# A gated recurrence in eight levels: its decay factors multiplied up beforehand, and GpSimd's product ordered behind VectorE's

## The chip, the cores and the metric

One NeuronCore of a Trainium2 chip runs the whole program. [...] The metric is the device time of one execution in microseconds (us); each kernel is timed several times and the median is taken.

## The reference, cut to what matters

One layer of a hybrid encoder block on 512 tokens of width 2048, in float32: an input norm, one wide projection, two token mixers, sigmoid gates, two projections merged, an output projection into the residual and a final norm. Mixer A, which the change touches, is a gated linear recurrence over 8 heads of 128:

```python
def step(state, inp):                       # one chunk of CHUNK tokens, g_c = log f
    q_c, k_c, g_c, v_c = inp
    cum = jnp.cumsum(g_c, axis=1)
    inter = jnp.einsum('bthk,bhkv->bthv', q_c * jnp.exp(cum), state)
    diff = cum[:, :, None] - cum[:, None, :]
    decay = jnp.exp(jnp.where(causal[None, :, :, None, None], diff, -jnp.inf))
    scores = jnp.einsum('bthk,bshk,btshk->bhts', q_c, k_c, decay)
    intra = jnp.einsum('bhts,bshv->bthv', scores, v_c)
    last = cum[:, -1]
    new_state = (jnp.exp(last)[..., None] * state
                 + jnp.einsum('bshk,bshv->bhkv', k_c * jnp.exp(last[:, None] - cum), v_c))
    return new_state, inter + intra
```

So a query at t meets a key at s with the product of the forget factors f between them. Mixer B is a sparse attention: an indexer scores all keys, the best 128 of them are kept for each query (top-k), and attention over those carries a position bias.

## The kernel before, in words

Nearly all the time goes into the projections. Their weights come from HBM in blocks (`wr`); ScalarE rounds a block to its high half (`wh`) and VectorE subtracts that for the low half (`wl`), and TensorE makes three matmuls of each product of halves. All other work is written as Python generators in "lanes" (`hgrn` for mixer A's recurrences, `top` for the top-k, `att` for the attention, `norm` and so on). The projection loops call `pump()` after some of their matmuls, and each `pump()` lets every lane emit its next piece. Nothing is reordered afterwards: the order in which pieces are emitted is the order of the instructions on each engine.

`hgrn_gen(p)` is one recurrence; it handles two heads (p = 3, 2, 0, 1 in the order of time). It holds q, k and f of two heads as tiles of 128 x 1024 (channels x 2 heads x 512 tokens: `hq`, `hk`, `hf`). The decay between a query and a key is not computed pair by pair but in levels 0 to 7. At level l, m = 2^(l-1) tokens make a half block. `scores(l, ps)` multiplies keys and queries as they stand into PSUM (`hl`, 16 to 64 small matmuls). Then `decay(l)` multiplies the later half of each block of q by the factor of the earlier half, on VectorE, and the earlier half of each block of k by the factor of the later half, on GpSimd, so that the next level's scores carry the right decay. The factors are in `tot`: one for each half block; neighbours multiplied together give the `tot` of the next level, half as long (512, 256, ... 8 columns). Level 0 has only the product of q with f, on VectorE. For levels below 6 VectorE then copies by a mask from PSUM into `hnear`; later levels are copied into `hS` by ScalarE. After level 7 the keys are transposed (`hkt`), chunk states are built (`hp`, `hst`; these use the last `tot`), outputs are made (`ho`) and normed (`hz`).

Between two levels stands one `yield`, so one pump: about 24 projection matmuls on TensorE.

The lane `top` is for VectorE alone: rounds of MAX and MATCH_REPLACE over 256, 384 or 512 columns of `M`. It is paced by `R.load`, the number of microseconds that the piece of the recurrence just emitted is reckoned to take on VectorE:

```python
while credit <= 0:
    yield
    credit += 2.7 - R.load
credit -= 0.4 + 0.27 * (b + 1)
```

Other names of the steps: `nt`, `ckh`, `ckl` (norm lane, during the first recurrence: a product on VectorE, its rounding on ScalarE, the difference on VectorE), `ak`, `av`, `aq` and `MB` (attention, during the last recurrence: `MB` is a sum of the bias on GpSimd).

Of the kernel before, what the change touches and what calls it, by code (L numbers as in the profile page):

```python
# [26 lines left out]
F32 = mybir.dt.float32  # L27
FR = mybir.dt.float32r
AF = mybir.ActivationFunctionType
OP = mybir.AluOpType  # L30
# [20 lines left out]
def hybrid_block(ctx, tc, x, norm_w, w_in, lb_table, gnorm_a, q_norm_w, kv_norm_w, w_uq,  # L51
# [3 lines left out]
    V, A, G, PE, SP = nc.vector, nc.scalar, nc.gpsimd, nc.tensor, nc.sync  # L55
# [12 lines left out]
    def bank(name):  # L68
        return sdp.tile([128, 512], F32, name=name, tag="sd")

    def split(hi, lo, src):
        A.activation(hi, src, AF.Copy)  # L72
        V.tensor_tensor(lo, src, hi.bitcast(F32), op=OP.subtract)  # L73
# [6 lines left out]
    def mm(ps, l, r, first, last):  # L80
        PE.matmul(ps, l, r, start=first, stop=last, skip_group_check=True)  # L81
# [34 lines left out]
    R = SimpleNamespace(load=0.0)  # L116
# [564 lines left out]
    def place(p, shape, dtype, name, tag):  # L681
        if p == 1 or tag not in ("hf", "hk", "hq"):
            return R.h.tile(shape, dtype, name=name, tag=tag)
        return R.i.tile(shape, dtype, name=name, tag=f"{tag}{p or 3}")
# [58 lines left out]
    def aq_evac(p):  # L743
        def evac(c, ps):
            if c == 0:
                hg[p, "q"] = place(p, [128, 2, T], F32, "hq", "hq")
            q = hg[p, "q"][:, c, :]
            A.activation(q, ps, AF.Sigmoid)
            V.scalar_tensor_tensor(q, ps, 128 ** -0.5, q, op0=OP.mult, op1=OP.mult)
            if c == 1:  # L750
                lanes["hgrn"].append(hgrn_gen(p))
        return evac

    def hgrn_gen(p):
        f, k, q = (hg[p, n] for n in "fkq")
        gate = R.h.tile([128, 2, T], F32, name="hg")
        SP.dma_start(gate, gate_d[2 * p:2 * p + 2].rearrange("f p t -> p f t"))
        S = R.h.tile([128, 8, 128], F32, name="hS")
        near = R.h.tile([128, 8, 32], F32, name="hnear")
        G.memset(near, 0.0)  # L760
        qf, kf, tot = (a.rearrange("p c t -> p (c t)") for a in (q, k, f))
        yield

        def scores(l, ps):

            m = max(32, 1 << l >> 1)
            for n in range(8):
                for h in range(0, 128, m if l < 6 else 2 * m):
                    s = n * 128 + h
                    t = s if l < 6 else s + m  # L770
                    mm(ps[h:h + m, n * m:n * m + m], kf[:, s:s + m], qf[:, t:t + m], True, True)

        def decay(l):
            if l == 0:
                V.tensor_tensor(qf, qf, tot, op=OP.mult)
                return tot
            m = 1 << (l - 1)
            nb = 1024 // (2 * m)
            qv = qf.rearrange("p (n a m) -> p n a m", a=2, m=m)
            kv = kf.rearrange("p (n a m) -> p n a m", a=2, m=m)  # L780
            tv = tot.rearrange("p (n a) -> p n a", a=2)
            V.tensor_tensor(qv[:, :, 1, :], qv[:, :, 1, :],
                            tv[:, :, 0:1].to_broadcast([128, nb, m]), op=OP.mult)
            G.tensor_tensor(kv[:, :, 0, :], kv[:, :, 0, :],
                            tv[:, :, 1:2].to_broadcast([128, nb, m]), op=OP.mult)
            nt = R.h.tile([128, nb], F32, name=f"tot{l}", tag=f"tot{l % 2}")
            V.tensor_tensor(nt, tv[:, :, 0], tv[:, :, 1], op=OP.mult)
            return nt

        for l in range(8):  # L790
            R.load = (1.7, 2.5, 2.1, 1.8, 1.8, 1.7, 1.3, 1.3)[l]
            if l == 4:
                G.memset(S, 0.0)
            ps = bank("hl")
            scores(l, ps)
            tot = decay(l)
            if l < 6:
                V.copy_predicated(near, R.levels[:, l:l + 1, :].to_broadcast([128, 8, 32]),
                                  ps[:, 0:256].rearrange("p (n t) -> p n t", n=8))
            else:  # L800
                m = 1 << (l - 1)
                for h in range(0, 128, 2 * m):
                    A.activation(S[h:h + m, :, h + m:h + 2 * m],
                                 ps[h:h + m, 0:8 * m].rearrange("p (n t) -> p n t", n=8), AF.Copy)
            if l == 6:
                for h in range(0, 128, 32):
                    A.activation(S[h:h + 32, :, h:h + 32], near[h:h + 32], AF.Copy)
            yield

        R.load = 0.0  # L810
        kd = R.h.tile([128, 2, 3, 128], F32, name="hkd")
        for c in range(2):
            pt = bank("hkt")
            for j in range(3):
                PE.transpose(pt[:, j * 128:(j + 1) * 128], k[:, c, j * 128:(j + 1) * 128], R.ident)
            A.activation(kd[:, c], pt[:, :384].rearrange("p (j t) -> p j t", j=3), AF.Copy)
        yield
        while (p, "v") not in hg:
            yield
        R.load = 1.4  # L820
        v = hg[p, "v"]
        st = R.h.tile([128, 2, 3, 128], F32, name="hst")
        for c in range(2):
            pp = bank("hp")
            for j in range(3):
                mm(pp[:, j * 128:(j + 1) * 128], kd[:, c, j, :], v[:, j, c * 128:(c + 1) * 128],
                   j == 0, True)
            A.activation(st[:, c, 0, :], pp[:, 0:128], AF.Copy)
            for j in (1, 2):
                V.scalar_tensor_tensor(st[:, c, j, :], st[:, c, j - 1, :],  # L830
                                       tot[:, c * 4 + j:c * 4 + j + 1],
                                       pp[:, j * 128:(j + 1) * 128], op0=OP.mult, op1=OP.add)
        yield
        sq = place(p, [128, 2, T], F32, "hk", "hk")
        zs = []
        o = place(p, [128, 2, T], F32, "ho", "hf")
        for c in range(2):
            po = bank("ho")
            for j in range(4):
                sl = slice(j * 128, (j + 1) * 128)  # L840
                mm(po[:, sl], v[:, j, c * 128:(c + 1) * 128], S[:, 4 * c + j, :], j == 0, j == 0)
                if j:
                    mm(po[:, sl], st[:, c, j - 1, :], q[:, c, sl], False, True)
            A.activation(o[:, c], po, AF.Copy)
            A.activation(sq[:, c], po, AF.Square)
            R.load = 0.7 * c
            yield
            zs.append((place(p, [128, T], FR, "hzh", ("hkd", "hst")[c]),
                       place(p, [128, T], FR, "hzl", ("hq", "hS")[c])))
            split(*zs[c], sq[:, c])  # L850
        R.load = 0.7
        yield
        R.load = 0.0
        for c in range(2):
            ps = bank("hz")
            mm(ps, ones_r, zs[c][0], True, False)
            mm(ps, ones_r, zs[c][1], False, True)
            A.activation(sq[:, c], ps, AF.Ln, bias=eps, scale=1.0 / 128)
        A.activation(sq, sq, AF.Exp, scale=-0.5)
        yield  # L860
        R.load = 2.9
        for c in range(2):
            r = sq[:, c]
            V.scalar_tensor_tensor(r, o[:, c], c_gw, r, op0=OP.mult, op1=OP.mult)
            V.tensor_tensor(r, r, gate[:, c], op=OP.mult)
        yield
        R.load = 1.3
        for c in range(2):
            y = [place(p, [128, T], FR, f"hy{i}", (("hkd", "hst"), ("hq", "hS"))[i][c]) for i in range(2)]
            split(*y, sq[:, c])  # L870
            for i in range(2):
                late[1].append(lambda y=y[i], i=i, h=2 * p + c: SP.dma_start(ya_d[i, h], y.bitcast(F32)))
        yield


    at_ = {}

    def uq_evac(p):
# [323 lines left out]
    def end_index():  # L1202
        lanes["misc"].extend(waiting)
        drain("misc")
        leave("idx")
        leave("raws")
        R.h = enter("hgrn", side="right")
        lanes["hgrn"].extend((hgrn_gen(3), hgrn_gen(2)))
        lanes["norm"].append(norm_gen(R.ckv, 2, c_kvw, R.ckh, R.ckl))
        lanes["t5"].append(t5_gen())  # L1210
# [355 lines left out]
```

## Time and profile before

| | |
|---|---|
| median of 3 runs | 1365.66 us (1365.21 to 1366.12) |
| the profiled execution | 1364.76 us, of which the span from the first to the last instruction 1362.9 us |
| granted TensorE clock | 0.999 |
| TensorE, weight loads, VectorE, ScalarE, GpSimd busy in the span | 1347.1, 1250.5, 1075.5, 656.9, 81.5 us |

The four recurrences run beside projections. The first scores of each start at 685.5, 749.6, 810.0 and 883.1 us, and the last scores of the last one start at 910.6 us. The rows of a timeline below give start, length, engine, line, operation, tiles and shapes of an instruction, and in brackets how long its engine was idle before it and which instruction ended that. On VectorE the next instruction often starts some 0.07 us before the one ahead of it ends. Matmul rows of one kind are merged.

### The profile page before, as it was taken

Reading aid. Unit: us, or ns where it says so; the run is one execution under the profiler, and the core shown is the slowest. Engines: PE = TensorE matmul, PEld = TensorE weight load, DVE = VectorE, ACT = ScalarE, POOL = GpSimd, SP = SyncE. Lnnn points to the kernel's source line nnn. Section 1 sums busy time; section 2 is a strip of 40 time slices with the busy share of each in tenths; the row PEclk is TensorE's granted clock in tenths of the full one; section 3 lists DMA queues with packets and bytes.
Section 4 is the critical chain, followed back from the end, with each engine's and each line's share of the span. In section 5 each row is a group of like instructions: output and inputs, shape, how many; then the busy total and the mean of one; then the engine's idle time right before and its main releaser. Section 6 shows DMA issues by size and latency. Waiting matters only on the chain.

```text
span 1362.9 us, 26828 instructions
## 1 busy us (share of the span) xinstructions
PE 1347.1 (99%) x10940; PEld 1250.5 (92%) x10940; DVE 1075.5 (79%) x1741; ACT 656.9 (48%) x1054; POOL 81.5 (6%) x85
## 2 busy tenths in 40 slices
PE   8999999999999999999999999999999999999997
PEld 7888999999999999999999888888888888899996
DVE  7896889988898888886779989575556658899856
ACT  6555445445554444445744443645434334354444
POOL 2100000000000000000030303040101100000000
PEclk9999999999999999999999999999999999999999
DMA  6334345544444445446235423434856556643463
GB/s 207 94 109 139 98 151 160 164 142 140 131 148 117 133 139 155 140 140 206 63 103 153 127 80 109 134 108 149 299 163 204 197 174 219 209 145 119 164 239 139
DMA packets 145165, 204.79 MB, mean 150 GB/s; under 512 B 10585, under 2 KB 87058, under 8 KB 144914
## 3 DMA queue, kind: packets, MB, share of 16 engines
q1 hardware_dynamic: 144754, 202.82, 47.5%
q8 instruction: 86, 1.41, 0.4%
q14 instruction: 37, 0.30, 0.1%
q10 hardware_dynamic: 288, 0.26, 0.1%
HBM read 167.89 MB, written 35.15 MB: 149 GB/s over the span
## 4 chain that ended last, share of the span: by engine, by line
PE 95%; DVE 2%; ACT 1%; issue 0%; DMA 0%; SPq 0%; ACTq 0%
PE pp L76 15%; PE pp L77 15%; PE pp L78 15%; PE acc L76 14%; PE acc L78 13%; PE acc L77 13%; PE hl L81 1%; PE acc L81 1%; PE ho L81 1%; PE sc L76 1%; PE sc L77 1%; PE sc L78 1%; DVE wl L73 1%; PE pt L313 0%; PE hp L81 0%
## 5 line engine op out<-in xcount | busy, mean ns | idle before, releaser
L150 ACT ACTIVATE bh<-wr 128x768 fp32r<-128x768 f32 x128 | 108.2, 845 | 218.4 <-issue 105.4
L152 ACT ACTIVATE wh<-sv 128x512 fp32r<-128x512 f32 x256 | 151.8, 623 | 85.2 <-DVE sv L145 66.1
L73 DVE TENSOR_TENSOR wl<-wr,wh 128x1024 fp32r<-128x1024 f32 (+1 forms) x104 | 127.7, 1229 | 58.1 <-ACT wh L72 57.8
L76 PE MATMUL pp<-s,wh 128*128 128x256 f32 x624 | 172.3, 276 | 0.0
L77 PE MATMUL pp<-s,wh 128*128 128x256 f32 x624 | 172.3, 276 | 0.0
L78 PE MATMUL pp<-s,wl 128*128 128x256 f32 x624 | 172.3, 276 | 0.0
L153 DVE TENSOR_TENSOR bl<-wr,bh 128x768 fp32r<-128x768 f32 x128 | 122.3, 955 | 51.0 <-ACT bh L150 50.9
L154 DVE TENSOR_TENSOR wl<-sv,wh 128x1024 fp32r<-128x1024 f32 x128 | 156.5, 1223 | 7.3 <-ACT wh L152 1.1
L72 ACT ACTIVATE wh<-wr 128x1024 fp32r<-128x1024 f32 (+1 forms) x104 | 108.0, 1040 | 104.4 <-PE acc L77 60.0
L76 PE MATMUL acc<-xh,wh 128*128 128x512 f32 x304 | 121.5, 400 | 0.0
L78 PE MATMUL acc<-xh,wl 128*128 128x512 f32 x304 | 118.6, 390 | 0.0
L77 PE MATMUL acc<-xl,wh 128*128 128x512 f32 x304 | 118.5, 390 | 0.0
L77 PEld LDWEIGHTS pp<-s,wh 128*128 128x128 f32 x624 | 117.2, 188 | 0.0
L76 PEld LDWEIGHTS pp<-s,wh 128*128 128x128 f32 x624 | 117.1, 188 | 0.0
L78 PEld LDWEIGHTS pp<-s,wl 128*128 128x128 f32 x624 | 117.1, 188 | 0.0
L76 PE MATMUL pp<-xh,bh 128*128 128x256 f32 x416 | 114.9, 276 | 0.0
L78 PE MATMUL pp<-xh,bl 128*128 128x256 f32 x416 | 114.9, 276 | 0.0
L77 PE MATMUL pp<-xl,bh 128*128 128x256 f32 x416 | 114.9, 276 | 0.0
L76 PE MATMUL acc<-yh,wh 128*128 128x512 f32 x256 | 100.2, 391 | 0.0
L78 PE MATMUL acc<-yh,wl 128*128 128x512 f32 x256 | 99.7, 390 | 0.0
L77 PE MATMUL acc<-yl,wh 128*128 128x512 f32 x256 | 99.7, 390 | 0.0
L145 DVE TENSOR_TENSOR sv<-wr 128x512 f32<-128x512 f32 x128 | 87.8, 686 | 10.0 <-DMA wr<-in_w_in_dram 6.0
(391 smaller groups left out, 3688.8 us busy)
## 6 DMA issues: line engine op xcount, KB each, us to landing
wr<-in_w_in_dram SPq DMA_DIRECT2D x136, 512.0 KB, 3.6
wr<-in_w_out_dram SPq DMA_DIRECT2D x32, 512.0 KB, 3.7
mg<-gate_d SPq DMA_DIRECT2D x48, 256.0 KB, 4.5
gate_d<-c SPq DMA_DIRECT2D x44, 256.0 KB, 5.2
wr<-in_w_in_dram SPq DMA_DIRECT2D x36, 256.0 KB, 2.8
wr<-in_w_pa_dram SPq DMA_DIRECT2D x16, 512.0 KB, 6.1
wr<-in_w_pb_dram SPq DMA_DIRECT2D x16, 512.0 KB, 4.0
x<-in_x_dram SPq DMA_DIRECT2D x8, 512.0 KB, 4.2
```

The source lines that it names most:

```text
L72: A.activation(hi, src, AF.Copy)
L73: V.tensor_tensor(lo, src, hi.bitcast(F32), op=OP.subtract)
L76: PE.matmul(ps, lh, rh, start=first, stop=False, skip_group_check=True)
L77: PE.matmul(ps, lh, rl, start=False, stop=False, skip_group_check=True)
L78: PE.matmul(ps, ll, rh, start=False, stop=last, skip_group_check=True)
L81: PE.matmul(ps, l, r, start=first, stop=last, skip_group_check=True)
L145: V.tensor_tensor(sv[:, 0:2, :], b[:, 1:3, :], b[:, 0:1, :].to_broadcast([128, 2, 256]), op=OP.add)
L150: A.activation(bh, b[:, 1:4, :], AF.Copy)
L152: A.activation(vh[:, i:i + 2, :], sv[:, i:i + 2, :], AF.Copy)
L153: V.tensor_tensor(bl, b[:, 1:4, :], bh.bitcast(F32), op=OP.subtract)
L154: V.tensor_tensor(vl, sv, vh.bitcast(F32), op=OP.subtract)
```

## The change

The seven multiplications that make the `tot` of levels 2 to 8 (the last being what the chunk states use) are moved out of `decay` to the first piece of the generator, ahead of level 0. Each gets a tile of its own; they were two tiles in turn. GpSimd's product of a level is made to wait for VectorE's product of the same level. The `R.load` figures are set anew: 2.1 for the first piece, and smaller ones for levels 1 to 7.

```diff
         qf, kf, tot = (a.rearrange("p c t -> p (c t)") for a in (q, k, f))
+        tots = [tot, tot]
+        for l in range(1, 8):
+            tv = tots[l].rearrange("p (n a) -> p n a", a=2)
+            tots.append(R.h.tile([128, 512 >> (l - 1)], F32, name=f"tot{l}"))
+            V.tensor_tensor(tots[-1], tv[:, :, 0], tv[:, :, 1], op=OP.mult)
+        tot = tots[-1]
+        R.load = 2.1
         yield
...
         def decay(l):
             if l == 0:
-                V.tensor_tensor(qf, qf, tot, op=OP.mult)
-                return tot
+                V.tensor_tensor(qf, qf, tots[0], op=OP.mult)
+                return
...
-            tv = tot.rearrange("p (n a) -> p n a", a=2)
-            V.tensor_tensor(qv[:, :, 1, :], qv[:, :, 1, :],
-                            tv[:, :, 0:1].to_broadcast([128, nb, m]), op=OP.mult)
-            G.tensor_tensor(kv[:, :, 0, :], kv[:, :, 0, :],
-                            tv[:, :, 1:2].to_broadcast([128, nb, m]), op=OP.mult)
-            nt = R.h.tile([128, nb], F32, name=f"tot{l}", tag=f"tot{l % 2}")
-            V.tensor_tensor(nt, tv[:, :, 0], tv[:, :, 1], op=OP.mult)
-            return nt
+            tv = tots[l].rearrange("p (n a) -> p n a", a=2)
+            first = V.tensor_tensor(qv[:, :, 1, :], qv[:, :, 1, :],
+                                    tv[:, :, 0:1].to_broadcast([128, nb, m]), op=OP.mult)
+            then = G.tensor_tensor(kv[:, :, 0, :], kv[:, :, 0, :],
+                                   tv[:, :, 1:2].to_broadcast([128, nb, m]), op=OP.mult)
+            tc.add_manual_dep(then.ins, first.ins.name, BEHIND, reason="one port for both engines")
...
-            R.load = (1.7, 2.5, 2.1, 1.8, 1.8, 1.7, 1.3, 1.3)[l]
+            R.load = (1.7, 1.1, 1.1, 1.1, 1.1, 1.1, 0.7, 0.7)[l]
```

The order of the instructions on TensorE, ScalarE, GpSimd and SyncE stays as it was; on VectorE it changes in the four recurrences. Two places of VectorE and one of GpSimd:

VectorE at the start of the third recurrence, before (`hq<-hq,hf 128x1024` is the product of level 0, the next `hq` that of level 1):

```order
L73 TENSOR_TENSOR wl<-wr,wh 128x1024
L675 MAX m_9909<-M 128x8
L676 MATCH_REPLACE M<-m_9909,M 128x512
L775 TENSOR_TENSOR hq<-hq,hf 128x1024
L798 COPY_PREDICATED hnear<-levels,hl 128x256
L675 MAX m_9975<-M 128x8
L676 MATCH_REPLACE M<-m_9975,M 128x512
L73 TENSOR_TENSOR wl<-wr,wh 128x1024
L782 TENSOR_TENSOR hq<-hq,hf 128x512
```

and now:

```order
L73 TENSOR_TENSOR wl<-wr,wh 128x1024
L766 TENSOR_TENSOR tot_9918<-hf 128x512
L766 TENSOR_TENSOR tot_9920<-tot_9918 128x256
L766 TENSOR_TENSOR tot_9922<-tot_9920 128x128
L766 TENSOR_TENSOR tot_9924<-tot_9922 128x64
L766 TENSOR_TENSOR tot_9926<-tot_9924 128x32
L766 TENSOR_TENSOR tot_9928<-tot_9926 128x16
L766 TENSOR_TENSOR tot_9930<-tot_9928 128x8
L675 MAX m_9932<-M 128x8
L676 MATCH_REPLACE M<-m_9932,M 128x512
L782 TENSOR_TENSOR hq<-hq,hf 128x1024
L803 COPY_PREDICATED hnear<-levels,hl 128x256
```

All seven stand between the split of weights and the product of level 0; the top-k round ahead of that product stays, and the round behind it has moved on (behind the masked copy of level 1).

VectorE in the first recurrence from level 3 to level 4, before:

```order
L73 TENSOR_TENSOR wl<-wr,wh 128x1024
L782 TENSOR_TENSOR hq<-hq,tot_8469 128x128x4
L787 TENSOR_TENSOR tot_8550<-tot_8469 128x128
L798 COPY_PREDICATED hnear<-levels,hl 128x256
L597 SCALAR_TENSOR_TENSOR nt<-ckv,cols,rr 128x512
L73 TENSOR_TENSOR ckl<-nt,ckh 128x512
L782 TENSOR_TENSOR hq<-hq,tot_8550 128x64x8
```

and now:

```order
L73 TENSOR_TENSOR wl<-wr,wh 128x1024
L789 TENSOR_TENSOR hq<-hq,tot_8258 128x128x4
L803 COPY_PREDICATED hnear<-levels,hl 128x256
L597 SCALAR_TENSOR_TENSOR nt<-ckv,cols,rr 128x512
L73 TENSOR_TENSOR ckl<-nt,ckh 128x512
L789 TENSOR_TENSOR hq<-hq,tot_8260 128x64x8
```

Only `tot` is gone from between the product and the masked copy.

GpSimd in the first recurrence, its products of levels 1 to 4 with what they wait for, before:

```order
L784 TENSOR_TENSOR hk<-hk,hf 128x512 [waits DMAHW5_49,DMAHW0_49,PE_49]
L784 TENSOR_TENSOR hk<-hk,tot_8403 128x256x2 [waits DVE_49,PE_49,Pool_49]
L784 TENSOR_TENSOR hk<-hk,tot_8469 128x128x4 [waits DVE_49,PE_49,Pool_49]
L793 MEMSET hS 128x1024 [waits Activation_49]
L784 TENSOR_TENSOR hk<-hk,tot_8550 128x64x8 [waits DVE_49,PE_49,Pool_49]
```

and now:

```order
L791 TENSOR_TENSOR hk<-hk,hf 128x512 [waits DMAHW5_49,DMAHW0_49,DVE_49]
L791 TENSOR_TENSOR hk<-hk,tot_8256 128x256x2 [waits DVE_49,Pool_49]
L791 TENSOR_TENSOR hk<-hk,tot_8258 128x128x4 [waits DVE_49,Pool_49]
L798 MEMSET hS 128x1024 [waits Activation_49]
L791 TENSOR_TENSOR hk<-hk,tot_8260 128x64x8 [waits DVE_49,Pool_49]
```

The wait for TensorE's scores is gone as a wait of its own, since VectorE's product, which waits for them too, is now waited for. TensorE's scores of the next level in turn wait for GpSimd's product alone.

More of the change, by code (lines that the diff above doesn't have):

```diff
@@ L795, in hgrn_gen @@
             scores(l, ps)
-            tot = decay(l)
+            decay(l)
             if l < 6:
@@ L873, in hgrn_gen @@
         yield
+    BEHIND = mybir.DependencyInfo(mybir.DependencyClass.Sync, mybir.DependencyReason.DATA)
     at_ = {}
```

## Prediction

> **What bounds the kernel now.** I read the page first (busy time and the chain), then TensorE's busy time by stage, then the list of what TensorE waited for.
>
> The page, busy time of the engines and the chain by engine:
>
> ```profile
> PE 1347.1 (99%) x10940; PEld 1250.5 (92%) x10940; DVE 1075.5 (79%) x1741; ACT 656.9 (48%) x1054; POOL 81.5 (6%) x85
> PE 95%; DVE 2%; ACT 1%; issue 0%; DMA 0%; SPq 0%; ACTq 0%
> ```
>
> TensorE is busy for all but 15.8 of 1362.9 us, so only its idle time can shrink, and any new wait of it adds straight to the end. The stages (start:end, length, then busy us of TensorE, its weight loads, VectorE, ScalarE, GpSimd):
>
> ```profile
> 0.00:60.00 60.00, 54.01 (x332) 49.64 (x333) 44.30 (x111) 33.38 (x57) 11.31 (x15) 1.00 0.48 153
> ...
> 685.00:913.00 228.00, 225.43 (x2933) 196.00 (x2932) 187.65 (x339) 103.37 (x152) 49.55 (x39) 1.00 0.39 116
> ...
> 1340.00:1363.00 23.00, 15.63 (x92) 13.75 (x90) 12.30 (x24) 9.67 (x26) 0.00 (x0) 0.93 0.49 183
> ```
>
> The four recurrences lie in the middle one of these three stages (I call them R1 to R4 in the order of time). TensorE idles there for 2.57 us (228 less 225.43), and its waits (total, times, longest) name the same 2.5 us: the score matmuls `hl` behind VectorE's product `hq` or the instruction after it.
>
> ```profile
> PE hl L81 <- DVE hq L775: 1.1, 1, 1.1
> PE hl L81 <- DVE hq L782: 0.7, 2, 0.5
> PE hl L81 <- DVE tot L787: 0.7, 1, 0.7
> ```
>
> So the most that the change can win at the recurrences is 2.5 us, 0.19%. What it can lose has no such lid. The rest of the 15.8 us lies ahead of 60 us (6.0) and behind 1340 us (7.3), which the change doesn't touch.
>
> **GpSimd's product behind VectorE's.** First, what the two engines do to each other now, at level 1 of R1 and at one place in R4 (start, length, instruction; in brackets the idle time ahead of it and what ended it):
>
> ```profile
> 689.19 0.76 PE L81 MATMUL hl<-hq,hk 128*32 128x32 f32 x64
> 689.99 0.69 DVE L782 TENSOR_TENSOR hq<-hq,hf 128x512 f32<-128x512 f32 x1 [0.42 <-PE hl L81]
> 690.04 2.05 POOL L784 TENSOR_TENSOR hk<-hk,hf 128x512 f32<-128x512 f32 x1 [12.95 <-PE hl L81]
> 690.60 2.03 DVE L787 TENSOR_TENSOR tot<-hf 128x512 f32<-128x512 f32 x1
> ...
> 901.02 0.74 POOL L929 TENSOR_TENSOR MB<-M,bh 128x256 f32<-128x256 f32 x1
> 901.07 0.43 DVE L798 COPY_PREDICATED hnear<-levels,hl 128x256 f32<-128x256 uint8 x1
> ```
>
> They already take turns: GpSimd's product reaches only to 692.09, 1.41 us after `hq` ends at 690.68, and `tot`, which takes 0.68 us alone (below), is held until GpSimd is done. The masked copy, which has one input in PSUM, runs beside GpSimd unhurt. So the new wait saves nothing between the pair. It puts the hand-over of a semaphore between them: the scores end at 689.95 and GpSimd, waiting for them, starts at 690.04, so I count 0.1 us. And GpSimd, which could run while a late `hq` was still queued on VectorE, no longer can. Queued behind it on GpSimd are only the next level's product, a memset and R4's bias sums; waiting for it is TensorE's next `hl`.
>
> Where VectorE is free when the scores end, this costs nothing. In R2 (`hq` of level 0, then the scores of levels 1 and 2):
>
> ```profile
> 750.36 1.23 DVE L775 TENSOR_TENSOR hq<-hq,hf 128x1024 f32<-128x1024 f32 x1 [0.15 <-PE hl L81]
> 753.17 0.76 PE L81 MATMUL hl<-hq,hk 128*32 128x32 f32 x64
> 756.79 0.76 PE L81 MATMUL hl<-hq,hk 128*32 128x32 f32 x64
> ```
>
> Scores of level 1 end at 753.93; `hq` 0.7, hand-over 0.1, GpSimd 1.4 to 1.5 gives 756.2, and TensorE comes to the next scores at 756.79. The cover is the 24 projection matmuls that TensorE has between two levels. It lets `hq` be half a microsecond late. Until now, with GpSimd running at the same time, `hq` alone could start 2.1 us late (756.79 less 753.93 less 0.7) before TensorE noticed. So the thing to look for is a level where VectorE comes to `hq` late.
>
> That is so in R1 at levels 3, 5 and 7, where `hq` stands behind a split of weights (`wl`) that has itself waited for ScalarE:
>
> ```profile
> 698.25 1.17 POOL L784 TENSOR_TENSOR hk<-hk,tot 128x512 f32<-128x512 f32 x1 [2.76 <-PE hl L81]
> 698.34 2.15 DVE L73 TENSOR_TENSOR wl<-wr,wh 128x1024 fp32r<-128x1024 f32 x1 [0.40 <-ACT wh L72]
> 700.42 0.68 DVE L782 TENSOR_TENSOR hq<-hq,tot 128x512 f32<-128x512 f32 x1
> 701.24 0.75 PE L81 MATMUL hl<-hq,hk 128*32 128x32 f32 x64 [0.19 <-DVE hq L782]
> 701.57 0.73 DVE L597 SCALAR_TENSOR_TENSOR nt<-ckv,cols,rr 128x512 f32<-128x512 f32 x1
> ...
> 708.43 0.68 DVE L782 TENSOR_TENSOR hq<-hq,tot 128x512 f32<-128x512 f32 x1
> 709.26 0.70 PE L81 MATMUL hl<-hq,hk 128*32 128x32 f32 x32 [0.72 <-DVE tot L787]
> ...
> 714.10 1.05 POOL L784 TENSOR_TENSOR hk<-hk,tot 128x512 f32<-128x512 f32 x1 [2.49 <-PE hl L81]
> 714.76 1.47 DVE L73 TENSOR_TENSOR wl<-wr,wh 128x1024 fp32r<-128x1024 f32 x1 [3.12 <-ACT wh L72]
> 717.20 0.82 PE L815 MATMUL hkt<-ident,hk 128*128 128x128 f32 x6
> ```
>
> - Level 3: the split is no longer held (2.15 becomes 1.22), so `hq` ends at 700.2, but GpSimd then runs from 700.3 to 701.45. TensorE, there at 701.05, waits 0.45 instead of 0.19: +0.25.
> - Behind `hq` stand the masked copy and `nt`. `nt` is now met by GpSimd's product and held until 701.45; it ends at 702.0, as `tot` above ended 0.54 after GpSimd. ScalarE's rounding of `nt`, VectorE's difference and the `hq` of level 4 follow in a chain, and then GpSimd. Level 4: +0.25, an estimate from these margins, the time from `nt` to that `hq` taken as it is now.
> - Level 5: `hq` ends at 709.11 and TensorE goes on at 709.26, GpSimd's product having been done while the split ran. Now it follows `hq`, 0.1 and 1.05 to 1.17 us more, less a little that the shorter products ahead save: +0.9.
> - Level 7: the split takes 0.25 less, `hq` ends at 716.6, GpSimd at 717.75; the transposes `hkt` want `hk` at 717.20: +0.6.
>
> R1 costs 2.0 us. It rests on `nt` being held, which no row shows. A `tot` or split was held, the masked copy was not; `nt` has two SBUF operands like the former, so I take it as held. If it is not, the chain behind it comes earlier than now, levels 4 and 5 give 0.4 back together, and R1 costs 0.5. Ends: 0.5 and 2.4. [...]
>
> **The factors ahead of level 0.** Each recurrence gets seven VectorE instructions before its first `hq` and loses them between levels. Alone they take:
>
> ```profile
> 818.88 0.68 DVE L787 TENSOR_TENSOR tot<-hf 128x512 f32<-128x512 f32 x1
> 759.71 0.41 DVE L787 TENSOR_TENSOR tot<-tot 128x256 f32<-128x256 f32 x1
> 701.02 0.28 DVE L787 TENSOR_TENSOR tot<-tot 128x128 f32<-128x128 f32 x1
> 716.76 0.15 DVE L787 TENSOR_TENSOR tot<-tot 128x8 f32<-128x8 f32 x1
> ```
>
> The three sizes in between lie from 0.15 to 0.28 each, so the seven take 2.0 to 2.4; each needs the one before, so nothing overlaps: 2.2. What was spent between levels is freed where VectorE has time anyway. What counts is whether VectorE has 2.2 us to spare ahead of level 0.
>
> R1:
>
> ```profile
> 686.28 1.23 DVE L775 TENSOR_TENSOR hq<-hq,hf 128x1024 f32<-128x1024 f32 x1 [3.14 <-PE hl L81]
> ```
>
> VectorE idled for 3.14 us ahead of level 0, which covers the seven: nothing.
>
> R3 is the place where it has none:
>
> ```profile
> 804.39 1.22 DVE L73 TENSOR_TENSOR wl<-wr,wh 128x1024 fp32r<-128x1024 f32 x1 [1.52 <-ACT wh L72]
> ...
> 813.62 1.22 DVE L775 TENSOR_TENSOR hq<-hq,hf 128x1024 f32<-128x1024 f32 x1
> 814.89 0.76 PE L81 MATMUL hl<-hq,hk 128*32 128x32 f32 x64 [1.11 <-DVE hq L775]
> ...
> 816.47 1.89 DVE L73 TENSOR_TENSOR wl<-wr,wh 128x1024 fp32r<-128x1024 f32 x1
> 818.28 0.68 DVE L782 TENSOR_TENSOR hq<-hq,hf 128x512 f32<-128x512 f32 x1
> 819.11 0.75 PE L81 MATMUL hl<-hq,hk 128*32 128x32 f32 x64 [0.53 <-DVE hq L782]
> ```
>
> From 804.39 to 814.84 VectorE runs without a gap (no row there has an idle time), started by ScalarE, and TensorE already waits 1.11 us at the end. The order puts the seven into this stretch and leaves the same top-k round behind them. The wait becomes 3.3: +2.2. Behind it one top-k round goes and the split at 816.47 is no longer held, so the 0.53 nearly goes: -0.4. R3 costs 1.8 (1.5 to 2.4).
>
> R2: `hq` of level 0 ended at 751.59 and was wanted at 753.17, a slack of 1.6 plus 0.15 of idle; 2.2 is 0.5 more (0.2 to 0.7).
>
> R4:
>
> ```profile
> 884.48 1.22 DVE L775 TENSOR_TENSOR hq<-hq,hf 128x1024 f32<-128x1024 f32 x1
> 886.75 0.76 PE L81 MATMUL hl<-hq,hk 128*32 128x32 f32 x64
> ```
>
> `hq` ends at 885.70, a slack of 1.05; 2.2 would be 1.15 over it if VectorE had no idle time in the blocks ahead, and nothing if it had enough. It has some, so I take 0.2, and 0.3 for level 2, where the splits of keys now stand between two products and GpSimd follows late: 0.5 (0 to 1.2).
>
> The smaller figures for `R.load` only move top-k rounds forward to where they take the place of `tot`; TensorE, ScalarE and SP keep their order. Nothing.
>
> **Sum.** 2.0 + 0.5 + 1.8 + 0.5 = 4.8 us, between 2.2 and 6.7. The profiled run took 1364.76 (span 1362.9), 0.9 below the median of 1365.66; I add to the median: 1370.4, 0.35% slower, its own range 1367.9 (all low ends) to 1372.4 (all high ends).
>
> **Rivals.**
> - The waits come out at the low ends: `nt` runs beside GpSimd, R2 and R4 find slack. 2.2 to 2.7 us, 1368.2. For it: these are sub-microsecond margins. Against: R3's stretch without a gap.
> - Not slower: VectorE, freed of the held `tot` (2.03 against 0.68 above), is on time everywhere and the three waits vanish: 1363.1. It needs `hq` of R3's level 0 to be done by 813.78, 1.1 us sooner, with 2.2 us put ahead of it. That decides it, and nothing there is freed.
> - VectorE's lateness reaches the weight halves `wl`, and projection matmuls wait too: R2 to R4 each lose the whole 2.2, 1375. Against: no wait of TensorE for `wl` is in the list, and halves are prepared two blocks ahead.
>
> **How the numbers follow.** A measurement of this kernel tells about 0.2% (2.7 us) from no change. Forecast 0.70, low ends 0.18, not slower 0.07, halves late 0.05. Slower: 0.70 + 0.05 = 0.75; same: 0.18 + 0.04; faster by over 0.2% would take more than the idle time there: 0.03. The range, 1366.8 to 1373.0, takes in the low ends' upper part and the high end of 6.7 with a little beyond.
>
> **What would show it.** Right: at R3's level 1 `hl` waits about 3 us for `hq`; in R1 `hl` and `hkt` wait for GpSimd's `hk`, which did not occur before; no `tot` longer than 0.7. Wrong: GpSimd's products done before TensorE arrives at R1's levels 3, 5 and 7, or R3's wait still near 1.1.

## The result, and the profile after

The changed kernel takes 1372.44 us (median of 6 runs, 1371.99 to 1372.81) against 1365.53 us for the kernel before (6 runs beside them, 1365.04 to 1366.12): a ratio of 1.0051, 95% interval 1.0041 to 1.0061. It is 6.9 us slower. The prediction said 1370.4 us, 4.8 us slower, with 1366.8 to 1373.0 as its range: the sign and the place were right, the size was a third short. The sum's own high end was 6.7 us; the measured 6.9 lies inside the stated range only by the little that was added beyond it.

The page of the changed kernel, busy time and chain (PE is TensorE, PEld its weight loads, DVE VectorE, ACT ScalarE, POOL GpSimd, SP SyncE):

```profile
PE 1348.3 (98%) x10940; PEld 1250.9 (91%) x10940; DVE 1059.4 (77%) x1741; ACT 656.5 (48%) x1054; POOL 73.1 (5%) x85
PE 91%; DVE 5%; ACT 2%; issue 1%; POOL 1%; DMA 0%; SPq 0%; DVEq 0%; POOLq 0%; ACTq 0%
```

VectorE is 16.1 us less busy than before and GpSimd 8.4 us: the two hold each other less. In the mean a `tot` of 512 columns takes 0.68 us where it took 1.35, VectorE's `hq` by `tot` 0.69 where it took 0.94, GpSimd's `hk` by `tot` 1.13 where it took 1.46. Yet the share of the chain that goes by VectorE has risen from 2% to 5%, and GpSimd is in it now. The list of TensorE's waits in the changed kernel (in all, times, longest) says where:

```profile
PE hl L81 <- DVE hq L782: 4.7, 3, 3.9
PE hl L81 <- POOL hk L791: 2.8, 4, 1.5
PE hkt L820 <- POOL hk L791: 0.4, 1, 0.4
```

These waits come to 7.9 us against 2.5 before. (L782 is level 0's product now, L791 GpSimd's, L766 makes a `tot`.)

From the first scores of one recurrence to those of the next, and in R4 to its `hkt`, read from the timelines of both profiles:

| us | R1 | R2 | R3 | R4 | together |
|---|---|---|---|---|---|
| before | 64.07 | 60.45 | 73.13 | 31.41 | 229.06 |
| after | 65.79 | 61.07 | 77.74 | 32.56 | 237.16 |
| difference | +1.72 | +0.62 | +4.61 | +1.15 | +8.10 |
| forecast | +2.0 | +0.5 | +1.8 | +0.5 | +4.8 |

The spans differ by 7.6 us (1370.5 against 1362.9); ahead of R1 the profile after was 0.4 us quicker. R1 and R2 are as forecast. R3 took 2.8 us more than forecast, and that is most of the miss.

### The profile page after: what moved, and what is told of

It is laid out like the page before. It is cut to its first block, busy times and chain, and to the rows that moved or that the text cites. A ratio compares the mean times of both kernels' runs of the same rounds, so it can differ in the third digit from the quotient of the medians.

```text
span 1370.5 us, 26806 instructions
## 1 busy us (share of the span) xinstructions
PE 1348.3 (98%) x10940; PEld 1250.9 (91%) x10940; DVE 1059.4 (77%) x1741; ACT 656.5 (48%) x1054; POOL 73.1 (5%) x85
## 4 chain that ended last, share of the span: by engine, by line
PE 91%; DVE 5%; ACT 2%; issue 1%; POOL 1%; DMA 0%; SPq 0%; DVEq 0%; POOLq 0%; ACTq 0%
PE pp L76 15%; PE pp L78 15%; PE pp L77 15%; PE acc L76 13%; PE acc L78 12%; PE acc L77 12%; PE hl L81 1%; PE acc L81 1%; PE ho L81 1%; DVE wl L73 1%; PE sc L76 1%; PE sc L77 1%; PE sc L78 1%; DVE M L676 0%; DVE tot L766 0%
```

## Where R3's time went

VectorE's seven `tot` ahead of level 0 and TensorE's scores of levels 1 and 2, timeline of the changed kernel:

```profile
813.43 1.22 DVE L73 TENSOR_TENSOR wl<-wr,wh 128x1024 fp32r<-128x1024 f32 x1
814.57 0.69 DVE L766 TENSOR_TENSOR tot<-hf 128x512 f32<-128x512 f32 x1
815.29 1.65 DVE L766 TENSOR_TENSOR tot<-tot 128x256 f32<-128x256 f32 x6
...
818.25 1.22 DVE L782 TENSOR_TENSOR hq<-hq,hf 128x1024 f32<-128x1024 f32 x1
...
819.52 1.08 PE L81 MATMUL hl<-hq,hk 128*32 128x32 f32 x64 [3.90 <-DVE hq L782]
...
825.50 0.68 PE L81 MATMUL hl<-hq,hk 128*32 128x32 f32 x56
```

The seven take 2.3 us (the instruction behind them starts at 816.86), and the wait is 3.90 where it was 1.11: +2.8 (forecast +2.2). The 0.53 at level 2 is gone, as forecast. But from the scores of level 1 to those of level 2 there are 5.98 us without any wait. Before, the same work took 3.69 (814.89 to 819.11, less the wait of 0.53). So 2.3 us went where TensorE was never idle. The granted clock (the figure behind TensorE's busy time and count; start:end and length stand ahead, and the last two figures are the transfers') names the cause:

```profile
811.27:814.69 3.42, 3.42 (x89) 1.00 0.02 5
814.69:818.10 3.41, 0.93 (x9) 1.00 0.61 146
818.10:821.51 3.41, 1.99 (x68) 0.50 0.98 351
821.51:824.92 3.41, 3.41 (x18) 0.50 0.82 275
824.92:828.34 3.42, 3.42 (x88) 1.00 0.01 2
```

TensorE idled from 815.62 to 819.52; at 818.10 its clock fell to half, and it came back only at 824.92. The projection matmuls of one level, which hide all other work, ran at half speed. The sum of R3 is then 2.8 - 0.5 + 2.3 = 4.6. That the clock is the cause had still to be shown.

## The experiments

My theory: the two halves of the change each add their waits, and R3's long wait costs its own length and a fall of the clock besides. The rivals: the 2.3 us come from the new order of instructions, from the waits behind GpSimd, or from the work itself, not from the clock. Medians are given; the kernel before measured 1364.91 us beside the runs 1 to 4 and 1365.22 us beside 5 to 8. "Level 2" stands for the time from R3's level-1 scores to its level-2 scores.

### 1. The wait alone

```diff
-            V.tensor_tensor(qv[:, :, 1, :], qv[:, :, 1, :],
+            first = V.tensor_tensor(qv[:, :, 1, :], qv[:, :, 1, :],
...
-            G.tensor_tensor(kv[:, :, 0, :], kv[:, :, 0, :],
+            then = G.tensor_tensor(kv[:, :, 0, :], kv[:, :, 0, :],
...
+            tc.add_manual_dep(then.ins, first.ins.name, BEHIND, reason="one port for both engines")
```

> The kernel before with the new wait alone: GpSimd's product of a level waits for VectorE's, and tot stays between the levels. Theory A (three costs: GpSimd running late behind a late hq in R1 and R4; the seven multiplications ahead of level 0; TensorE's clock at half behind R3's long wait): this run has only the first of them, 1.7 us in R1 and some 0.7 in R4 as the changed kernel's trace has them, perhaps more, since tot now follows hq on VectorE and takes its turn ahead of GpSimd. 1367 to 1369.5 us, granted clock 1.00 throughout R3, R3 within 0.5 us of before. Rival B (the order of the two engines is what costs, also in R3): about 1372, with R3 some 4 us longer.

(The `reason` in the diff is a label in the code. No run here shows a port, only longer instructions where the two engines meet: `tot` of 512 columns took 1.35 us in the mean before, 0.68 after.)

1369.49 us, ratio 1.0038 (1.0025 to 1.0050). R1 +1.96, R2 0.00, R3 +1.23, R4 +1.03. In R1 the same three waits for `hk` as after the whole change (0.55, 1.55, 0.40). In R3, where no more than 0.5 us was expected, there is a wait at level 2 that the whole change does not have, since there `hq` is early enough (timeline of this run):

```profile
816.90 0.76 PE L81 MATMUL hl<-hq,hk 128*32 128x32 f32 x64 [1.12 <-DVE hq L775]
820.38 1.89 POOL L784 TENSOR_TENSOR hk<-hk,hf 128x512 f32<-128x512 f32 x1 [40.22 <-DVE hq L782]
822.32 0.76 PE L81 MATMUL hl<-hq,hk 128*32 128x32 f32 x64 [1.64 <-POOL hk L784]
```

The wait alone costs 4.6 us and saves no time.

### 2. The factors ahead, without the wait

```diff
-            tc.add_manual_dep(then.ins, first.ins.name, BEHIND, reason="one port for both engines")
```

> The changed kernel without the new wait: the seven multiplications stay ahead of level 0, GpSimd goes as soon as the scores are done. Theory A: R1 as before or a little better (no wait of hl for hk), R2 +0.6, R3 +4.6 with hl of level 1 waiting 3.9 us for hq and the clock at half behind it, R4 +0.3: 1370 to 1371.5 us. Rival B: near 1365.5.

1368.89 us, ratio 1.0029 (1.0018 to 1.0039): 4.0 us, of which R3 has 3.57. That is 1.1 us below what was expected, because R3 lost less than after the whole change. The long wait and the slow level are there without the manual dependency:

```profile
817.63 1.08 PE L81 MATMUL hl<-hq,hk 128*32 128x32 f32 x64 [3.88 <-DVE hq L782]
822.65 0.76 PE L81 MATMUL hl<-hq,hk 128*32 128x32 f32 x64
```

Level 2 took 5.02 us, 1.3 over the usual 3.7 and not 2.3: the half clock lasted 3.4 us here and 6.8 us after the whole change. The parts, 4.2 us (the wait alone) and 4.6 us (factors ahead) in the recurrences, together are 8.8; the whole change has 8.1. That they nearly add up is partly luck: run 1's wait of 1.64 us is not in the whole change, and run 2's half clock lasted half as long.

### 3. The changed kernel with more work in the wait

Twelve matmuls of 512 columns go ahead of R3's level-1 scores, into the bank that these then overwrite.

```diff
+            if (p, l) == (0, 1):
+                for _ in range(12):
+                    mm(ps, ones_r, xh[0][:, 0, :], True, True)
             scores(l, ps)
```

> The changed kernel with twelve more matmuls of 512 columns on TensorE ahead of the scores of R3's level 1; their result is overwritten by the scores. They need nothing that is late, and about 0.24 us each, so they fill some 2.8 us of the 3.9 us in which TensorE stood idle, and hl still waits for the same hq. Theory A (the clock falls because TensorE is idle for long): granted clock 1.00 in R3, the scores of level 2 come 3.7 us after those of level 1 instead of 6.0, 1372.4 less 2.3 = 1370.1 us although TensorE has more to do. Rival C (the slow 6 us come from something else there, transfers or VectorE's order): no change, 1372.4.

1370.88 us (1369.89 to 1370.97), ratio 1.0041 (1.0027 to 1.0055), against 1.0051 (1.0041 to 1.0061) of the changed kernel: with twelve matmuls more, it is 6.0 us above the kernel before measured beside it, where the changed kernel is 6.9 (2.3 less was expected). The two intervals overlap, so the profile has to carry the verdict. Its timeline, and then a stretch with its clock (as above):

```profile
816.42 2.90 PE L81 MATMUL hl<-xh,ones_r 128*128 128x512 f32 x12
820.48 0.76 PE L81 MATMUL hl<-hq,hk 128*32 128x32 f32 x64 [1.16 <-DVE hq L782]
824.19 0.76 PE L81 MATMUL hl<-hq,hk 128*32 128x32 f32 x64
```

```profile
819.00:823.00 4.00, 2.84 (x81) 1.00 1.00 354
```

The scores of level 1 come just as late as in the changed kernel (7.6 us after those of level 0, as there), so VectorE's delay is untouched; what filled the wait was useless work. Level 2 takes 3.71 us, the clock stays at 1.00, and R3 is 2.3 us shorter (75.43 against 77.74). So the 2.3 us are the clock's, and they come of the idleness: the order of instructions and the waits behind GpSimd are the same here.

### 4. and 5. Only the delay, in two sizes

The kernel before, with the seven multiplications put ahead of level 0 in R3 alone, their results unused; then only the first two of them (`range(1, 3)` in the diff).

```diff
+        if p == 0:
+            extra = [tot, tot]
+            for l in range(1, 8):
+                ev = extra[l].rearrange("p (n a) -> p n a", a=2)
+                extra.append(R.h.tile([128, 512 >> (l - 1)], F32, name=f"extra{l}", tag=f"tot{l % 2}"))
+                V.tensor_tensor(extra[-1], ev[:, :, 0], ev[:, :, 1], op=OP.mult)
```

> The kernel before with seven more multiplications on VectorE ahead of level 0 of R3 alone, the same as the changed kernel has there; their results are not used, and tot is still made between the levels. Theory A: hl of level 1 waits 1.1 + 2.3 = 3.4 us, the clock falls to half behind it, and the time is 1365.5 + 2.3 + 2.3 - 0.5 = 1369.6 us. Rival C: +2.3 alone, 1367.8.

> The kernel before with only the first two of the seven extra multiplications ahead of level 0 of R3 (results not used). hl of level 1 waits 1.1 + 1.1 = 2.2 us. Theory A: in the changed kernel the clock fell 2.8 us after TensorE had stopped, so 2.2 us leave it at 1.00; level 2 comes 3.7 us after level 1, and the whole costs 1.1 less what the wait at level 2 gives back: before +0.6 to +1.1 us. Rival D (any wait of a few us lowers the clock, in proportion): some +1.7 with a part of R3 below 1.00.

The seven: 1368.64 us (1367.31 to 1369.92), ratio 1.0028 (1.0017 to 1.0038). R3 is 3.37 longer and nothing else moves by more than 0.1. The two: 1366.74 us (1365.88 to 1368.44), ratio 1.0011 (1.0002 to 1.0020), R3 +1.07. Its median is 1.5 us above the kernel before, where 0.6 to 1.1 was expected; the profile, of an execution of 1366.58 us, shows where the clock was in that one alone. First the run with seven, its timeline and the windows with the clock; then the same of that with two:

```profile
817.70 0.76 PE L81 MATMUL hl<-hq,hk 128*32 128x32 f32 x64 [3.40 <-DVE hq L781]
822.94 0.76 PE L81 MATMUL hl<-hq,hk 128*32 128x32 f32 x64
```

```profile
815.84:819.25 3.41, 1.55 (x71) 1.00 1.00 328
819.25:822.66 3.41, 3.41 (x18) 0.50 0.59 199
```

```profile
816.53 0.76 PE L81 MATMUL hl<-hq,hk 128*32 128x32 f32 x64 [2.17 <-DVE hq L781]
```

```profile
811.88:815.29 3.41, 2.48 (x22) 1.00 0.33 74
815.29:818.70 3.41, 2.17 (x76) 1.00 0.97 289
```

The wait of 3.40 us is 1.11 plus 2.29, what the seven take. The clock fell in this profile only 1.5 us after the wait had ended. A wait of 2.17 us left it alone. (The 2.8 us in the expectation of run 5 are 2.5 by the rows of the changed kernel: TensorE stopped at 815.62 and the clock fell at 818.10.)

### 6. A version meant to mend it

The seven stand behind level 0's product, and the reckoned load keeps the top-k rounds out of that piece; the rest is as in the changed kernel.

```diff
...
-            R.load = (1.7, 1.1, 1.1, 1.1, 1.1, 1.1, 0.7, 0.7)[l]
+            R.load = (3.8, 1.1, 1.1, 1.1, 1.1, 1.1, 0.7, 0.7)[l]
...
+            if l == 0:
+                factors()
+                tot = tots[-1]
```

> The changed kernel with the seven multiplications behind VectorE's product of level 0 instead of ahead of it. VectorE has the same to do; in R3 its lateness falls on two waits, 1.1 us at level 1 and some 2.3 at level 2, neither long enough for the clock by theory A. So R3 +1.8 instead of +4.6, R2 less than +0.6, R1 some +2 (the product of level 1 is now behind the seven), R4 +1: 1370 us, 2.4 below the changed kernel. Rival C: 1372.4 as the changed kernel.

1372.61 us, ratio 1.0054 (1.0041 to 1.0068): a miss, no better than the change. Level 1's product comes late instead of level 0's, GpSimd follows it, and R1 has a new wait of 1.20 us. In R3 two waits took the place of one (timeline, then windows with the clock):

```profile
817.96 0.76 PE L81 MATMUL hl<-hq,hk 128*32 128x32 f32 x64 [1.61 <-DVE hq L783]
823.90 0.76 PE L81 MATMUL hl<-hq,hk 128*32 128x32 f32 x64 [2.15 <-POOL hk L792]
829.14 0.76 PE L81 MATMUL hl<-hq,hk 128*32 128x32 f32 x64
```

```profile
821.52:824.93 3.41, 1.26 (x68) 1.00 1.01 356
824.93:828.34 3.41, 3.41 (x18) 0.50 0.04 13
```

After a wait of only 2.15 us the clock fell, and the level behind it took 5.24 us; after 2.17 us in run 5 it did not fall. The length of the wait is not what decides.

### 7. and 8. The waits that were there before

Run 7 is the kernel before with the top-k round ahead of R3's level 0 held back; run 8 has besides, in the norm lane, VectorE's difference one piece behind ScalarE's rounding.

```diff
+        if p == 0:
+            R.load = 2.7
         yield
...
-            split(hi[:, j, :], lo[:, j, :], t)
+            A.activation(hi[:, j, :], t, AF.Copy)
+            yield
+            V.tensor_tensor(lo[:, j, :], t, hi[:, j, :].bitcast(F32), op=OP.subtract)
```

> The kernel before with R.load = 2.7 in the first piece of R3, so that the top-k round ahead of its level 0 (1.5 us on VectorE) is emitted later. Theory A: hl of level 1 no longer waits and level 2 waits 0.5 at most: -1.1 to -1.6 us, 0.1%. If VectorE's lateness only moves on, 0.

> As d7, and in the norm lane the subtraction behind ScalarE's rounding of nt is emitted one piece later, so that R1's products of levels 4 and 5 no longer stand behind a VectorE instruction that waits for ScalarE. Theory A: R1's 0.7 us at level 5 goes too: -1.8 to -2.3 us against before, 0.15%. If the chain through ScalarE sets level 5 in any case, as d7.

Run 7: 1363.88 us, ratio 0.9990 (0.9981 to 0.9999); R3's wait of 1.11 is gone. Run 8: 1363.53 us, ratio 0.9987 (0.9978 to 0.9996), the lowest median of all kernels here, 1.7 us below the kernel before (1.8 to 2.3 expected) and 8.9 us below the changed one; the intervals of runs 7 and 8 overlap. Its waits of `hl` are this one line:

```profile
PE hl L81 <- DVE hq L786: 0.7, 2, 0.5
```

In the recurrences its profile is 1.5 us shorter than that of the kernel before (227.59 against 229.06): more than half of the 2.5 us that the prediction named as all there was to win there, got by moving a round and a subtraction, without touching the factors.

### 9. and 10. When the clock falls

The kernel before, with VectorE's product of levels 0, 2, 4 and 6 followed by multiplications by one, in numbers that differ from place to place and between the two runs (run 9's are shown).

```diff
+        ones = R.h.tile([128, 512], F32, name="ones")
+        G.memset(ones, 1.0)
+        again = {3: (3, 6, 7, 8), 2: (3, 7, 6, 5), 0: (2, 8, 6, 7), 1: (3, 6, 8, 6)}[p]
...
+                for _ in range(again[0]):
+                    V.tensor_tensor(qf, qf, ones[:, 0:1].to_broadcast([128, 1024]), op=OP.mult)
...
+                ov = ones[:, :nb].rearrange("p (n a) -> p n a", a=1)
+                for _ in range(again[l // 2]):
+                    V.tensor_tensor(qv[:, :, 1, :], qv[:, :, 1, :],
+                                    ov.to_broadcast([128, nb, m]), op=OP.mult)
...
+            if l % 2 == 0:
+                R.load += 0.7 * again[l // 2]
```

> The kernel before, with VectorE's product of levels 0, 2, 4 and 6 followed by further multiplications of the same elements by one (k of them: 2 or 3 of about 1.23 us at level 0, 5 to 8 of about 0.69 us at the others), so that TensorE has to wait at 16 places by about 0.8 + 0.69 k - 2.84 us: 1.4 for k = 5, 2.1 for 6, 2.8 for 7, 3.5 for 8, and 2.2 for k = 3 at level 0, each between levels that run as before. It asks when the granted clock falls. Theory A (the clock is judged over windows of one fixed length that run on whatever the program does): the starts of all falls lie at whole multiples of one period of about 3.4 us from each other, each fall lasts one or two such periods, and whether a wait of about 2 us brings one depends on how it lies against them: some of the waits of 2.1 and 2.8 us do, others of the same length do not. Theory B (the clock falls when an idle time passes a length of about 2.8 us): every wait of 3.5 us brings a fall 2.8 us after its beginning, none of 2.1 does, and the distances between falls fit no period. Time by both: about 16 x 2.3 = 37 us of waits, and 1.4 to 1.7 us for each fall, 4 to 12 of them: 1408 to 1424.

> As the run with waits at 16 places, with other numbers of repeated multiplications (k = 2 to 4 at level 0, 5 to 8 at levels 2, 4 and 6, in another order), so that other lengths meet other moments. Theory A (windows of a fixed length): again one period of about 3.4 us between all falls, and waits of 2 to 3 us on both sides. Theory B (length of the idle time alone): the same limit as in the other run divides the waits that bring a fall from those that do not, to 0.2 us. Time by both 1405 to 1422.

1471.07 and 1466.89 us, one time of each. The times missed by some 45 us, of which one wait of 24.8 and 24.9 us is the larger part: the raised load held top-k rounds back, and they ran in a row ahead of R4's level 0. The other waits came out longer than reckoned, too (up to 5.0 us). For the question this does not matter. Reading the granted clock by quarters of a microsecond, run 9 has 15 falls in the recurrences. Counted from the first (691.94) the others begin 7, 11, 25, 28, 32, 36, 49, 52, 56, 60, 77, 87, 90 and 95 times 3.413 us later, each to within 0.03 us; the 13 falls of run 10 lie on one such grid as well (0, 4, 20, 24, 28, 32, 46, 53, 56, 72, 82, 86, 91). All but those of the 24.8 us last 3.41 or 6.83 us. The other runs agree: in the changed kernel a fall at the start begins at 12.55 us, 236 windows of 3.413 us ahead of that at 818.10. Theory A holds in all of these: the falls lie on windows of 3.413 us (run 9's last fall is 324.27 us, 95 of them, behind its first) that run on whatever the program does.

With the grid known, every window of the recurrences (680 us on) can be laid against the clock of the next. On both sides of the limit (three pairs of windows of run 10, then one of run 9):

```profile
697.24:700.65 3.41, 1.43 (x13) 1.00 0.00 0
700.65:704.07 3.42, 2.27 (x70) 0.50 0.02 5
...
850.84:854.25 3.41, 1.64 (x15) 1.00 0.65 147
854.25:857.67 3.42, 0.59 (x64) 1.00 0.99 344
...
864.49:867.91 3.42, 1.49 (x14) 1.00 0.00 0
867.91:871.32 3.41, 2.04 (x75) 1.00 0.02 5
```

```profile
985.50:988.91 3.41, 1.55 (x68) 1.00 0.02 5
988.91:992.33 3.42, 3.42 (x10) 0.50 0.00 0
```

TensorE busy for 1.43 us of a window, 42% of it: the next one is at half clock. Busy for 1.49: it is not. From there to 1.6 us the order is blurred. The last window above, busy for 1.55, brought a fall, and so did run 4's with 1.55; these two have 68 and 71 matmuls, the spared one of 1.49 us has 14. Whether the number of matmuls decides there is not shown. In the recurrences of the six profiles compared so (the changed kernel, runs 2, 4, 6, 9 and 10) no window with less than 1.43 us of work was spared and none with more than 1.6 was punished. At the start of the program this does not hold throughout: in run 4 the window from 3.46 to 6.87 us, on the same grid, has 1.26 us of work, and the next one reads 1.00. A window at half clock gave the full one back when TensorE was busy for 88% of it or more (3.01 of 3.41 us, changed kernel, 12.55 to 15.96), and kept the half when for 82% or less (2.80 of 3.42 us, run 10, 782.57 to 785.99). Now the earlier runs fall into place: run 6's 2.15 us lay within one window (1.26 of it busy, above); run 5's 2.17 were cut by a boundary (2.48 and 2.17 busy).

## Why the prediction was right, and where its size was off

- **R1, +2.0 forecast, +1.72 measured: right.** The estimate rested on `nt` being held by GpSimd. It is: 1.60 us here, 0.73 before (timeline after):

```profile
699.77 1.15 POOL L791 TENSOR_TENSOR hk<-hk,tot 128x512 f32<-128x512 f32 x1 [4.49 <-DVE hq L789]
699.87 1.60 DVE L597 SCALAR_TENSOR_TENSOR nt<-ckv,cols,rr 128x512 f32<-128x512 f32 x1
...
700.97 0.76 PE L81 MATMUL hl<-hq,hk 128*32 128x32 f32 x64 [0.55 <-POOL hk L791]
...
709.99 0.70 PE L81 MATMUL hl<-hq,hk 128*32 128x32 f32 x32 [1.53 <-POOL hk L791]
...
718.59 0.88 PE L820 MATMUL hkt<-ident,hk 128*128 128x128 f32 x6 [0.41 <-POOL hk L791]
```

  Against before: level 3 0.55 for 0.19 (+0.36, forecast +0.25), level 5 1.53 for 0.72 (+0.8, forecast +0.9), `hkt` +0.4 (forecast +0.6). Of level 4's +0.25 only 0.10 came: GpSimd was done there at 704.70, and the scores start at 704.75 after 0.10 us of idle time. Run 1 shows that all of this is the manual dependency's.
- **R2, +0.5 forecast, +0.62 measured: right.** One wait of 0.62 us for level 0's product; run 2, with the factors ahead alone, has +0.50.
- **R3, +1.8 forecast with 1.5 to 2.4 as its bounds, +4.61 measured: the term that was mis-sized.** The step that failed is "The wait becomes 3.3: +2.2": a wait was priced at its own length. The wait was 3.90: 2.3 for the seven, as forecast, and 0.5 more. In run 4, the seven alone, it is 3.40, so the 0.5 belongs to the rest of the change; 0.4 of it can be read, since VectorE's unbroken stretch ahead of level 0 was released by ScalarE 5.20 us ahead of the scores (806.73 to 811.93) where it had been 5.6 (804.39 to 810.00). Above all, the fall of the clock took 2.3 us more (run 3), of which the prediction knew nothing.
- **R4, +0.5 forecast, +1.15 measured: right in place, inside its bounds of 0 to 1.2.** Waits of 0.17, 0.37 and 0.36 us; the latter two are for GpSimd's product, and with the wait alone (run 1) R4 has +1.03. With the factors ahead alone (run 2) it has +0.25. So GpSimd behind VectorE, not the lateness of level 0, makes most of it. Ahead of the last of the three, GpSimd's product stood behind two of the bias sums `MB` (2.92 us) and a memset on its own queue.
- **"The new wait saves nothing between the pair": right.** `tot` is never held now, and VectorE's 16 us less of busy time buy nothing, because they were not on the path.

The sum would have been 7.1 with R3's clock added; that the total still fell inside the range, with R3 out of its bounds, is partly luck. Of the rivals, the low ends' 1368.2 lies below every execution of the changed kernel; "not slower" needed level 0 of R3 sooner, and it came later; and halves late did not occur, since no wait of TensorE for `wl` is in the list (its 1375 is 1374.3 by its own terms, 2.0 and three times 2.2).

## What to carry to other kernels

Where TensorE is the bound, a wait of it is not priced by its length alone: in these runs, once it took about 2 us out of one of the clock's 3.4 us windows, the next window or two ran at half speed, 1.3 to 2.3 us on top. Worked out from the limits of 1.43 and 1.6 us above, which is an estimate: a wait under 1.8 us would not bring that by itself (the rest of its window is then over 1.6 us of work); one of 3.9 us nearly always would (split by a boundary, one side still has 1.95 idle and 1.46 of work); in between it depends on where the boundary falls (2.15 us brought a fall in run 6, 2.17 none in run 5). And before an engine's work is ordered behind another's to spare both, look at who was waiting for the second one: being held by each other was free here, being last was not.

## What the runs showed that was not expected

Useless matmuls in a wait made a stretch faster: twelve of them, 2.9 us of TensorE's time, saved 2.3 us in R3 (run 3); on the whole kernel that is too little for its interval to leave that of the changed kernel. Half the clock comes with a delay, up to 1.5 us after the wait that brought it has ended (run 4), so that a stretch without a single wait shows the loss and the list of waits does not. And moving VectorE's lateness by one level to where it has less slack turned one wait into two with the same fall behind them (run 6).
